# A hybrid S5 and mLSTM trunk on one core: where two weight blocks are staged, weight splits in pieces, and the step at which the W2 maxima are taken

## The chip, the cores and the metric

The kernel runs on one core of a Trainium2 chip. The metric is the device time of one execution in microseconds (us), of which the median over runs is taken. The engines are named as the profile does: PE (TensorE, matrix products), DVE (VectorE), ACT (ScalarE), POOL (GpSimd) and SP (SyncE, which here only issues DMAs).

## The reference

One layer of a streaming encoder on x of 2048 tokens by 1024 channels, float32. Its two mixers, S5 groups with a GLU and mLSTM heads, give 512 columns each:

```python
h = rmsnorm(x, norm_mix_g[l])
p = h @ w_in[l]
u, q_raw, k_raw, v, o_raw, i_raw, f_raw = jnp.split(p, cuts, axis=-1)
y_ssm = s5_mixer(u, ...)      # scan, GELU, z * sigmoid(z @ w_glu + b_glu), rmsnorm
y_ml = mlstm_mixer(q_raw, k_raw, v, o_raw, i_raw, f_raw, ...)
x = x + jnp.concatenate([y_ssm, y_ml], axis=-1) @ w_out[l]
h = rmsnorm(x, norm_ffn_g[l])
x = x + jnp.square(jax.nn.relu(h @ w_ff1[l])) @ w_ff2[l]
...
return rmsnorm(x, final_norm_g)
```

W_out is 1024 by 1024; W1 is 1024 by 4096 and W2 4096 by 1024.

## The kernel before

**Products.** Every float32 product is made of float16 parts: a weight w and an operand are each split into a high part and the rest (hi, lo), and three matmuls add up hi·hi, hi·lo and lo·hi (`mm3`, L160 to L162, and `mmx`, L1398 to L1400 in the FFN). So that the parts don't overflow, each weight block is first scaled by a power of two from the largest magnitude in it. Preparing a block is therefore: DMA of float32 into SBUF; the maximum of its magnitudes on DVE; a maximum over the partitions through PE and DVE (`all_max`, L94 to L101, tiles `pmx_...` and `ma_...`); some one-column steps; hi on ACT and lo on DVE.

**Mixers and the hand-over (to about 720 us).** The mixers go through 16 chunks of tokens. GLU steps (`glu_step(n)`, tiles `zc`, `pz`, `zt`, `pgl`, `gth`, `pgT`, `ms`; 128 tokens of one n at a time) run beside them and after them: `zt` is the split GLU input, `pgl` its product with W_glu, and `pgT` transposes the finished columns into `ms`, the operand of the output projection. The last chunk of the mLSTM (`og`, `pT`, `mo`, `mix_store`) fills the other half of it and writes it to DRAM (`ml_d`), from where it comes back as `hop0ml`, `hop1ml`. The output projection (`out_proj`, bank `po`, eight tiles of 128 output columns by 512 tokens, 24 matmuls each) adds its result to the x tiles `x2` (L1057).

**W_out** lies in four blocks of 256 columns. `load_wo(i)` calls `load_w` (L127 to L149), which takes a staging tile from the pool `stg` of one buffer (128 x 2048 float32, 1 MB), loads into it (L130), takes the maxima (`w_scale`, L107), and splits it in 8 pieces (L141 on ACT, L142 on DVE). Blocks 0 and 1 come during chunks 13 and 14 (L975, L977), block 2 before the last chunk's store (L979), and block 3 later, ahead of GLU step 9 (L1334). Two tiles of `po` use one block. The x tiles are four accumulators of 1 MB each, `accx`, tags `ax0` to `ax3`, loaded by `load_acc` (L1003 to L1005).

**FFN (about 830 to 2125 us).** Two phases over the halves of the tokens. A phase has 16 W1 blocks (numbered u below) of 128 x 2048 float32, each followed by its part of W2 (two halves of a load `r2`), in a scheme of seven products on sums of quarter blocks. Raw weights are combined on POOL (L1278 to L1281 for W1, L1319 to L1322 for W2), then split by `w_split` (L1263 to L1265: hi L1264 on ACT, lo L1265 on DVE) into `wA` and `wC` of 1024 columns, `wB` of 1536, and the `w2o` operands of 512 or 768. `f_scale` takes the maximum over the 2048 columns of one block (L1203 to L1212, tiles `m1_a..`, `m1_b..`, on DVE L1205) for those that aren't measured ahead; a stands for W1, b for W2. PE's results of the first product (`fx`, `fv`, `fw`) become the hidden operand (tiles `e..`, `t2f` L1101 and L1105, split on ACT L1090 and POOL L1091); the second (`gx`, `gv`, `gw`) is evacuated by DVE into the x tiles (L1494, in `f2_mp`), and only then does PE get its bank back. While phase 0 runs, DVE and POOL also prepare the operands of the second half of the tokens (tiles `b..`, L1142 to L1155, and `ho`), until about 1400 us.

`f2_mp` is a generator; for each quarter step qd and each product i of seven it issues the matmuls, the evacuations, and then at certain steps the preparation of what comes next: `w2_prep` of the next quarter step at i = 0, `w2_load` of the next pair of blocks at i = 1 of even qd, and `w2_scale` (which calls `f_scale`) of that pair at i = 6 of even qd.

**What sets the order.** The rows of all engines are set at build time by a scheduler that simulates the engines. So an edit in one place can move instructions elsewhere, and the order that came out is static.

Of the kernel before, what the change touches and what calls it, by code (L numbers as in the profile page):

```python
# [43 lines left out]
O_GMIX, O_GFFN, O_GFIN, O_GOUT, O_CW, O_CB, O_D, O_BI, O_BF, NCOL = 0, 8, 16, 24, 32, 64, 72, 104, 105, 106  # L44
# [3 lines left out]
def trunk(  # L48
# [18 lines left out]
    nc = tc.nc  # L67
    V, S, G, T = nc.vector, nc.scalar, nc.gpsimd, nc.tensor
# [7 lines left out]
    smal = ctx.enter_context(pool("smal", bufs=3))  # L76
# [50 lines left out]
    def load_w(src, K, N, ga, name, slot=0, wp=None, tag=None, E=V, st=None):  # L127
        if st is None:
            st = stg.tile([P, K, N], F32, name=f"st_{name}", tag="stg")
            nc.sync.dma_start(out=st, in_=src)  # L130
        wt = (wp or wpool).tile([P, 2, K, N], F16, name=f"w_{name}", tag=tag or f"w{slot}")
        sg, mp = w_scale(st, K, N, ga, name)
        if ga is not None and E is G:
            for k in range(K):
                V.tensor_scalar(out=st[:, k, :], in0=st[:, k, :], scalar1=sg[:, k:k + 1], scalar2=None, op0=ALU.mult)
                if k % 2 == 1:
                    S.activation(out=wt[:, 0, k - 1:k + 1], in_=st[:, k - 1:k + 1], func=AF.Copy)
                    G.tensor_tensor(out=wt[:, 1, k - 1:k + 1], in0=st[:, k - 1:k + 1], in1=wt[:, 0, k - 1:k + 1], op=ALU.subtract)
        elif ga is not None:
            for k in range(K):  # L140
                S.activation(out=wt[:, 0, k, :], in_=st[:, k, :], func=AF.Copy, scale=sg[:, k:k + 1])  # L141
                V.scalar_tensor_tensor(out=wt[:, 1, k, :], in0=st[:, k, :], scalar=sg[:, k:k + 1], in1=wt[:, 0, k, :], op0=ALU.mult, op1=ALU.subtract)  # L142
# [778 lines left out]

    wo, r_w = [None] * 4, [None] * 4

    def load_wo(i, slot=0, wp=None, tag=None):
        wo[i], m = load_w(wout[i], KD, 256, O_GOUT, f"out{i}", slot, wp, tag)
        r_w[i] = descale(m, 2.0 ** -24, f"out{i}", tag="dsw")

    mix_load(0)
# [7 lines left out]
    for b in range(16):  # L936
# [39 lines left out]
            load_wo(0, 2)  # L976
        if b == 14:  # L977
            load_wo(1, 0)
    load_wo(2, 1)  # L979
    mix_store(15)  # L980
    r_ctx.close()

# [214 lines left out]
    def sc1(name):  # L1197
        return scal.tile([P, 1], F32, name=name)
# [2 lines left out]

    def f_scale(raw, nm):

        m1 = smal.tile([P, 1], F32, name=f"m1_{nm}", tag="w_m1")
        V.tensor_reduce(out=m1, in_=raw, axis=AX.X, op=ALU.max, apply_absolute_value=True)  # L1205
        ma = all_max(m1, nm, *psx[nm[0]])
        mp = sc1(f"fm_{nm}")
        V.tensor_scalar(out=ma, in0=ma, scalar1=1e-30, scalar2=None, op0=ALU.max)
        V.tensor_scalar(out=mp.bitcast(I32), in0=ma.bitcast(I32), scalar1=0x7F800000, scalar2=None, op0=ALU.bitwise_and)
        sg = sc1(f"fs_{nm}")  # L1210
        V.reciprocal(sg, mp)
        V.tensor_scalar(out=sg, in0=sg, scalar1=4096.0, scalar2=None, op0=ALU.mult)  # L1212
        return mp, sg
# [47 lines left out]
                mp1["g", u // 2] = mg  # L1261

    def w_split(hi, lo, src, sg):  # L1263
        S.activation(out=hi, in_=src, func=AF.Copy, scale=sg)  # L1264
        V.scalar_tensor_tensor(out=lo, in0=src, scalar=sg, in1=hi, op0=ALU.mult, op1=ALU.subtract)  # L1265
# [31 lines left out]
    def w2_scale(ph, v):  # L1297
        raw = raw2[ph, v]
        if ph == 0:
            mp, sg2[v] = scanned.get(("b", v)) or f_scale(raw.rearrange("p m s n -> p (m s n)"), f"b{v}")  # L1300
            dd = dd2[v] = sc1(f"dd{v}")
            mg = mp1["g", v // 2]
            V.tensor_scalar(out=dd, in0=mg, scalar1=mg, scalar2=Mg2, op0=ALU.mult, op1=ALU.mult)
            V.tensor_scalar(out=dd, in0=dd, scalar1=mp, scalar2=None, op0=ALU.mult)

    def w2_prep(ph, q, wp=None, tag=None):
        v, j = q // 2, q % 2
        raw, sg = raw2[ph, v], sg2[v]
# [12 lines left out]
        G.tensor_tensor(out=r[:, 2], in0=r[:, 0], in1=r[:, 2], op=ALU.subtract)
        G.tensor_tensor(out=r[:, 1], in0=r[:, 1], in1=s12[:, 1], op=ALU.subtract)  # L1322
        w_split(fl(w[:, 0, 5:7]), fl(w[:, 1, 5:7]), fl(s12), sg)
        w_split(fl(w[:, 0, 2:5]), fl(w[:, 1, 2:5]), fl(r[:, 1:4]), sg)
        wops2[ph, q] = {n: w[:, :, i] for i, n in enumerate(("A11", "A12", "S4", "S3", "A22", "S1", "S2"))}


    def load_ml(t):
        mlr[t] = new_hop(t, f"ml{t}").rearrange("p a (b h) t -> p (a b) h t", h=2)
        nc.sync.dma_start(out=mlr[t], in_=ml_d[t])  # L1330

    load_ml(0)
    load_acc(0)
    load_wo(3, wp=r3, tag="wo3")  # L1334
    glu_step(9)
    for n in range(10, NGL):
        if n in (10, 12, 14):
            load_acc((n - 8) // 2)
        if n == 13:
            load_ml(1)  # L1340
        out_proj(0, n - 10)
        glu_step(n)
# [138 lines left out]
    def f2_mp(ph, g, mp, fam):  # L1481
        qd = 4 * g + mp
        nm = f"{ph}{qd}"
        dd = dd2[qd // 2]
        bk = {}
        acc = accx[mp]
        w = wops2[ph, qd]
        nq = (ph, qd + 1) if qd + 1 < 32 else (1, 0) if ph == 0 else None
        for i, (b, wn, op) in enumerate(PR2):
            if b not in bk:  # L1490
                bk[b] = bank(fam + b, f"g{b}{nm}")
            mmx(bk[b], [(w[wn][:, 0, f * P:(f + 1) * P], w[wn][:, 1, f * P:(f + 1) * P], hid[ph, 2 * g + f, op][:, 0, :], hid[ph, 2 * g + f, op][:, 1, :]) for f in range(2)], first=(i in (0, 1, 5)), last=True)
            for j, c in ((0, 0),) if i in (0, 5) else ((1, 1),) if i in (1, 4) else ((0, 1),) if i in (2, 3) else ((1, 0),):
                V.scalar_tensor_tensor(out=acc[:, j, c, :], in0=bk[b], scalar=dd, in1=acc[:, j, c, :], op0=ALU.mult, op1=ALU.add)  # L1494
            if i == 0 and nq:
                w2_prep(*nq)
            nv = (ph, qd // 2 + 1) if qd // 2 + 1 < 16 else (1, 0) if ph == 0 else None
            if i == 1 and qd % 2 == 0 and nv:
                w2_load(*nv)
            if i == 6 and qd % 2 == 0 and nv:  # L1500
                w2_scale(*nv)
            yield
        if ph == 0 and g == NFB // 2 - 1:
            for c in range(2):
                if accf[c] is None:
                    accf[c] = r3.tile([P, TB], F32, name=f"accf{ph}{c}", tag="acc", bufs=2)
# [198 lines left out]
```

## Time and profile before

| | |
|---|---|
| median of 3 runs | 2147.97 us (2147.96 to 2151.23) |
| the profiled execution | 2149.39 us |
| its span, first to last instruction | 2147.7 us |
| mean granted clock of TensorE | 0.979 |
| busy: PE, DVE, ACT, POOL | 2033.2, 1688.4, 1090.1, 1086.1 us |
| DMA | 176.57 MB, mean 82 GB/s |

A row of a timeline has the start in us, the length in us (for several instructions in a row, xcount, of them all), the engine, the line, the operation, what it writes and reads, its shape, and in brackets how long the engine was idle before it and what it was waiting for. Lines are those of the program above. A window has for each engine the busy time and the number of instructions in it, then the clock that TensorE was granted, the share of the DMA engines and their rate.

### The profile page before, as it was taken

The page shows a single profiled execution, that of the slowest core. Times are in us where ns is not written, and L with a number is a line of the kernel's source. Part 1 is how long each engine was busy: PE and PEld are TensorE (multiplying, and loading weights), DVE is VectorE, ACT ScalarE, POOL GpSimd, SP SyncE. Part 2 cuts the span into 40 slices and gives each one's busy share as a digit, 9 for nine tenths or more (in the row PEclk, how much of TensorE's full clock was granted, in tenths as well). Part 3 has the DMA queues.
Part 4 walks back from the last instruction along what each step waited for, and adds up shares of the span by engine and source line. Part 5 has one row for each costly group of instructions (what it writes and reads, how often), then busy time and mean ns, then how long its engine had stood idle before and what let it go on. Part 6 is the DMA issues. An engine that isn't in the chain of part 4 may idle for free.

```text
span 2147.7 us, 30032 instructions
## 1 busy us (share of the span) xinstructions
PE 2033.2 (95%) x11205; PEld 1160.0 (54%) x11205; DVE 1688.4 (79%) x2820; ACT 1090.1 (51%) x2078; POOL 1086.1 (51%) x988
## 2 busy tenths in 40 slices
PE   6999898998999799999999999999999999999996
PEld 4986776776667454444444444444444444444445
DVE  8878888887857766757988989987887887777776
ACT  6436555555545422365544554555655555555543
POOL 2124446453211102576765776685776567565645
PEclk9999999999999899999999999999999999999998
DMA  5112112211103342312222222125433232121112
GB/s 189 51 52 60 50 40 47 70 35 57 60 21 113 113 196 78 118 45 69 94 69 83 80 94 80 63 79 196 138 137 103 100 112 79 40 79 43 36 40 79
DMA packets 56883, 176.57 MB, mean 82 GB/s; under 512 B 8032, under 2 KB 21536, under 8 KB 43168
## 3 DMA queue, kind: packets, MB, share of 16 engines
q1 hardware_dynamic: 56736, 174.65, 24.1%
q8 instruction: 88, 1.44, 0.3%
q14 instruction: 59, 0.48, 0.1%
HBM read 137.83 MB, written 28.41 MB: 77 GB/s over the span
## 4 chain that ended last, share of the span: by engine, by line
PE 58%; DVE 23%; POOL 6%; DMA 5%; ACT 4%; issue 3%; SPq 1%; POOLq 0%; DVEq 0%; ACTq 0%
PE fx L1400 4%; PE fx L1398 3%; PE fx L1399 3%; PE gx L1398 3%; PE gx L1400 3%; PE gx L1399 3%; PE po L160 3%; PE po L162 3%; PE po L161 3%; DVE w2o L1265 2%; DMA r<-in_w_dram 2%; DVE x L1494 2%; PE fv L1400 2%; PE fv L1399 2%; PE fv L1398 2%
## 5 line engine op out<-in xcount | busy, mean ns | idle before, releaser
L1399 PEld LDWEIGHTS <-w2o 128*128 128x128 f16 x952 | 93.5, 98 | 125.8 <-issue 29.2
L1427 ACT ACTIVATE e<-e 128x512 f32<-128x512 f32 x96 | 60.3, 628 | 197.6 <-DVE e L1463 96.2
L1398 PEld LDWEIGHTS <-w2o 128*128 128x128 f16 x952 | 93.8, 98 | 104.4 <-issue 2.6
L1400 PEld LDWEIGHTS <-w2o 128*128 128x128 f16 x952 | 93.6, 98 | 103.7 <-DVE w2o L1265 2.4
L162 PE MATMUL pv<-w_vo,xn 128*128 128x256 f16 x512 | 142.5, 278 | 2.5 <-DVE vx L440 2.5
L160 PE MATMUL pv<-w_vo,xn 128*128 128x256 f16 x512 | 142.3, 278 | 1.0 <-ACT xn L449 1.0
L161 PE MATMUL pv<-w_vo,xn 128*128 128x256 f16 x512 | 142.3, 278 | 0.0
L1264 ACT ACTIVATE w2o<-r,fs_b 128x512 f16<-128x512 f32 (+1 forms) x96 | 78.9, 824 | 113.8 <-POOL r L1322 52.6
L1265 DVE SCALAR_TENSOR_TENSOR w2o<-r,fs_b,w2o 128x512 f16<-128x512 f32 (+1 forms) x96 | 103.9, 1084 | 26.1 <-ACT w2o L1264 25.7
L1322 POOL TENSOR_TENSOR r<-r,s 128x256 f32<-128x256 f32 x64 | 65.2, 1021 | 105.7 <-DVE w2o L1265 104.3
L1494 DVE SCALAR_TENSOR_TENSOR x2b<-gx,dd,x2b 128x512 f32<-128x512 f32 x112 | 82.8, 745 | 42.6 <-PE gx L1400 42.3
L1494 DVE SCALAR_TENSOR_TENSOR x<-gx,dd,x 128x512 f32<-128x512 f32 x128 | 94.4, 742 | 12.2 <-PE gx L1400 11.9
L1278 POOL TENSOR_TENSOR s<-r 128x512 f32<-128x512 f32 x32 | 52.8, 1650 | 91.5 <-issue 64.6
L160 PE MATMUL pq<-xn,w_qk 128*128 128x512 f16 x256 | 97.6, 382 | 0.0
L161 PE MATMUL pq<-xn,w_qk 128*128 128x512 f16 x256 | 97.6, 381 | 0.0
L162 PE MATMUL pq<-xn,w_qk 128*128 128x512 f16 x256 | 97.5, 381 | 0.0
L1398 PE MATMUL fx<-hop,wB 128*128 128x512 f16 x256 | 97.0, 379 | 0.1
L1399 PE MATMUL fx<-hop,wB 128*128 128x512 f16 x256 | 97.0, 379 | 0.0
L1400 PE MATMUL fx<-hop,wB 128*128 128x512 f16 x256 | 97.0, 379 | 0.0
L162 PEld LDWEIGHTS <-xn 128*128 128x128 f16 x768 | 88.0, 115 | 11.9 <-DVE vx L440 2.7
L160 PEld LDWEIGHTS <-xn 128*128 128x128 f16 x768 | 88.2, 115 | 11.3 <-ACT xn L449 1.7
L161 PEld LDWEIGHTS <-xn 128*128 128x128 f16 x768 | 88.2, 115 | 9.7 <-issue 0.7
(1373 smaller groups left out, 6948.6 us busy)
## 6 DMA issues: line engine op xcount, KB each, us to landing
r<-in_w_dram SPq DMA_DIRECT2D x64, 1024.0 KB, 5.0
xt<-in_xN_dram SPq DMA_DIRECT2D x16, 512.0 KB, 4.4
rt<-rh SPq DMA_DIRECT2D x64, 128.0 KB, 2.3
hopd<-ho SPq DMA_DIRECT2D x28, 256.0 KB, 2.5
hop<-hopd SPq DMA_DIRECT2D x7, 1024.0 KB, 5.0
st_vo<-in_wvo_dram SPq DMA_DIRECT2D x4, 1024.0 KB, 5.1
bcm<-negM_d SPq DMA_DIRECT2D x16, 256.0 KB, 3.2
ml_d<-mo SPq DMA_DIRECT2D x16, 256.0 KB, 2.3
```

The costliest lines, as they stand in the source:

```text
L160: T.matmul(out, wh, xh, start=(i == 0), stop=False)
L161: T.matmul(out, wh, xl, start=False, stop=False)
L162: T.matmul(out, wl, xh, start=False, stop=(i == n - 1))
L1264: S.activation(out=hi, in_=src, func=AF.Copy, scale=sg)
L1265: V.scalar_tensor_tensor(out=lo, in0=src, scalar=sg, in1=hi, op0=ALU.mult, op1=ALU.subtract)
L1278: G.tensor_tensor(out=s12[:, 0], in0=raw[:, 2], in1=raw[:, 3], op=ALU.add)
L1322: G.tensor_tensor(out=r[:, 1], in0=r[:, 1], in1=s12[:, 1], op=ALU.subtract)
L1398: T.matmul(out, wh, xh, start=(first and i == 0), stop=False, skip_group_check=True)
L1399: T.matmul(out, wh, xl, start=False, stop=False, skip_group_check=True)
L1400: T.matmul(out, wl, xh, start=False, stop=(last and i == n - 1), skip_group_check=True)
L1427: S.activation(out=x, in_=x if src is None else src, func=AF.Relu, scale=scale)
L1494: V.scalar_tensor_tensor(out=acc[:, j, c, :], in0=bk[b], scalar=dd, in1=acc[:, j, c, :], op0=ALU.mult, op1=ALU.add)
```

## The change

Three edits.

1. W_out blocks 2 and 3 no longer use the buffer `stg`. Two tiles of the tags `ax2` and `ax3` of the x accumulators take them; both are loaded by DMAs issued in front of `load_acc(0)`, and x tiles 2 and 3 load into these slots after the splits. `load_wo(2)` moves from ahead of `mix_store(15)` to behind it, `load_wo(3)` from ahead of `glu_step(9)` to behind it. The buffer `stg` is free for W1 block 0 earlier.
2. `f_scale` takes its maximum in two halves of 1024 columns and a third reduction over the two; `w_split` works in pieces of at most 512 columns (1024 in two, 1536 in three, 768 in 512 and 256), each with its ACT and DVE instruction.
3. In `f2_mp`, `w2_scale` moves from product 6 of an even quarter step to product 0 of the odd one after it, and `w2_prep` of the odd ones from product 0 to product 1.

```diff
-    def load_wo(i, slot=0, wp=None, tag=None):
-        wo[i], m = load_w(wout[i], KD, 256, O_GOUT, f"out{i}", slot, wp, tag)
+    def load_wo(i, slot=0, wp=None, tag=None, st=None):
+        wo[i], m = load_w(wout[i], KD, 256, O_GOUT, f"out{i}", slot, wp, tag, st=st)
...
-    load_wo(2, 1)
     mix_store(15)
...
     def f_scale(raw, nm):
 
+        mx = smal.tile([P, 8], F32, name=f"mx_{nm}", tag="w_mx")
+        for o in range(2):
+            V.tensor_reduce(out=mx[:, o:o + 1], in_=raw[:, 1024 * o:1024 * o + 1024], axis=AX.X, op=ALU.max, apply_absolute_value=True)
         m1 = smal.tile([P, 1], F32, name=f"m1_{nm}", tag="w_m1")
-        V.tensor_reduce(out=m1, in_=raw, axis=AX.X, op=ALU.max, apply_absolute_value=True)
+        V.tensor_reduce(out=m1, in_=mx[:, 0:2], axis=AX.X, op=ALU.max)
...
     def w_split(hi, lo, src, sg):
-        S.activation(out=hi, in_=src, func=AF.Copy, scale=sg)
-        V.scalar_tensor_tensor(out=lo, in0=src, scalar=sg, in1=hi, op0=ALU.mult, op1=ALU.subtract)
+        n = src.shape[-1]
+        for o in range(0, n, 512):
+            c_ = slice(o, min(o + 512, n))
+            S.activation(out=hi[:, c_], in_=src[:, c_], func=AF.Copy, scale=sg)
+            V.scalar_tensor_tensor(out=lo[:, c_], in0=src[:, c_], scalar=sg, in1=hi[:, c_], op0=ALU.mult, op1=ALU.subtract)
...
+    st_o = []
+    for i in (2, 3):
+        st_o.append(accxp.tile([P, KD, 256], F32, name=f"st_o{i}", tag=f"ax{i}"))
+        nc.sync.dma_start(out=st_o[-1], in_=wout[i])
     load_ml(0)
     load_acc(0)
-    load_wo(3, wp=r3, tag="wo3")
+    load_wo(2, 1, st=st_o[0])
     glu_step(9)
+    load_wo(3, wp=r3, tag="wo3", st=st_o[1])
...
-            if i == 0 and nq:
+            if qd % 2 == 0 and i == 0:
                 w2_prep(*nq)
...
-            if i == 6 and qd % 2 == 0 and nv:
-                w2_scale(*nv)
+            if qd % 2 == 1 and nq:
+                if i == 0:
+                    w2_scale(ph if qd < 31 else 1, nq[1] // 2)
+                elif i == 1:
+                    w2_prep(*nq)
```

The change moves rows on all engines. Lines after the edits are numbered a few higher in the changed program (L1265 is L1270 there, L1105 is L1104, L1494 is L1504). The first place is the hand-over. PE before, from the last products of GLU step 9 (`pgl9`) to the first output projection (`po00`):

```order
L913 MATMUL pT15_8163<-ident_72,og33_7898 128x128
L98 MATMUL pmx_gm_8195<-ident_72,gm_8193 128x128
L913 MATMUL pT15_8163<-ident_72,og33_7898 128x128 x3
L98 MATMUL pmx_out3_8220<-ident_72,m1_out3_8218 128x128
L806 MATMUL pgT7_8249<-ident_72,zc7_7791 128x128 x4
L160 LDWEIGHTS w_out0_7447
L160 MATMUL po00_8292<-ms0_6491,w_out0_7447 128x512
L160 LDWEIGHTS w_out0_7447
...
L775 MATMUL pz10_8258<-ident_72,zc10_8256 128x128 x4
L806 MATMUL pgT8_8320<-ident_72,zc8_7958 128x128 x4
L161 LDWEIGHTS w_out0_7447
L161 MATMUL po00_8292<-ms0_6491,w_out0_7447 128x512
```

And now:

```order
L913 MATMUL pT15_8126<-ident_72,og33_7898 128x128
L98 MATMUL pmx_gm_8158<-ident_72,gm_8156 128x128
L98 MATMUL pmx_out2_8185<-ident_72,m1_out2_8183 128x128
L913 MATMUL pT15_8126<-ident_72,og33_7898 128x128 x3
L806 MATMUL pgT7_8214<-ident_72,zc7_7791 128x128 x4
L160 LDWEIGHTS w_out0_7447
L160 MATMUL po00_8292<-ms0_6491,w_out0_7447 128x512
L160 LDWEIGHTS w_out0_7447
...
L775 MATMUL pz10_8223<-ident_72,zc10_8221 128x128 x4
L98 MATMUL pmx_out3_8260<-ident_72,m1_out3_8258 128x128
...
L161 MATMUL po00_8292<-ms0_6491,w_out0_7447 128x512
```

`pgT7`, which is followed by the first matmuls of the output projection, stood behind `pmx_out3`; now `pmx_out2` stands there, and `pmx_out3` comes after the transposes. DVE at the same place, where `zt9` is the operand of `pgl9`, before:

```order
L789 SCALAR_TENSOR_TENSOR gth8_8116<-pgl8_8103,zd_6522,bg_6514 128x512
...
L772 TENSOR_SCALAR zc9_8093<-uz1_1023,zs_6521 128x512
...
L791 SCALAR_TENSOR_TENSOR zc8_7958<-gth8_8116,zc8_7958 128x512
L810 TENSOR_TENSOR ms0_6491<-pgT6_8086,ms0_6491 128x8x64
...
L778 TENSOR_TENSOR zt9_8100<-pz9_8095,zt9_8100 128x512
...
L797 TENSOR_SCALAR zc8_7958<-zc8_7958,vg8_8120,zo_6523 128x512
...
L107 TENSOR_REDUCE mx_out3_8215<-st_out3_8212 128x8
...
L810 TENSOR_TENSOR ms0_6491<-pgT7_8249,ms0_6491 128x8x64
```

And now, with the maxima `mx_out2`, `mx_out3` and those of W1 block 0, `mx_a0`:

```order
L107 TENSOR_REDUCE mx_out2_8180<-st_o2_8171 128x8
L789 SCALAR_TENSOR_TENSOR gth8_8116<-pgl8_8103,zd_6522,bg_6514 128x512
...
L772 TENSOR_SCALAR zc9_8093<-uz1_1023,zs_6521 128x512
L107 TENSOR_REDUCE mx_out3_8255<-st_o3_8173 128x8
L1205 TENSOR_REDUCE mx_a0_8918<-r1_00_8809 128x1 x2
...
L895 SCALAR_TENSOR_TENSOR og33_7898<-og33_7898,pn151_8065 128x256
L810 TENSOR_TENSOR ms0_6491<-pgT6_8086,ms0_6491 128x8x64
L791 SCALAR_TENSOR_TENSOR zc8_7958<-gth8_8116,zc8_7958 128x512
L778 TENSOR_TENSOR zt9_8100<-pz9_8095,zt9_8100 128x512
...
L810 TENSOR_TENSOR ms0_6491<-pgT7_8214,ms0_6491 128x8x64
```

Three more reductions now stand ahead of the row that writes `zt9`, and no maximum of a weight block between it and the row that writes `ms0` from `pgT7`.

The second place is DVE in the FFN at W1 block 4, around the second `t2f04` row, which waits for POOL. Before:

```order
L1494 SCALAR_TENSOR_TENSOR x2_1_8289<-gx05_10951,dd2_10619,x2_1_8289 128x512
L1265 SCALAR_TENSOR_TENSOR wB05_10948<-r1_05_10379,sg_a4a5b2b3_9089,wB05_10948 128x1536
L1265 SCALAR_TENSOR_TENSOR w2o06_10959<-r2_03_10832,sg_a4a5b2b3_9089,w2o06_10959 128x512
L1494 SCALAR_TENSOR_TENSOR x2_1_8289<-gv05_10982,dd2_10619,x2_1_8289 128x512
L1265 SCALAR_TENSOR_TENSOR w2o06_10959<-s2_06_10962,sg_a4a5b2b3_9089,w2o06_10959 128x512
L1105 TENSOR_TENSOR t2f04_10898<-b2104_10938,t2f04_10898 128x512
L1155 TENSOR_TENSOR b41_0_10262<-b40_0_10757,b41_0_10262 128x512
L1494 SCALAR_TENSOR_TENSOR x2_1_8289<-gx05_10951,dd2_10619,x2_1_8289 128x512
L1205 TENSOR_REDUCE m1_a7_11033<-r1_07_10996 128x1
```

And now:

```order
L1504 SCALAR_TENSOR_TENSOR x2_1_8289<-gx05_11017,dd2_10700,x2_1_8289 128x512
L1270 SCALAR_TENSOR_TENSOR wB05_11010<-r1_05_10423,sg_a4a5b2b3_9100,wB05_11010 128x512
L1504 SCALAR_TENSOR_TENSOR x2_0_8177<-gx04_10854,dd2_10700,x2_0_8177 128x512
L1270 SCALAR_TENSOR_TENSOR wB05_11010<-r1_05_10423,sg_a4a5b2b3_9100,wB05_11010 128x512 x2
L1104 TENSOR_TENSOR t2f04_10963<-b2104_11000,t2f04_10963 128x512
L1154 TENSOR_TENSOR b41_0_10300<-b40_0_10818,b41_0_10300 128x512
L1270 SCALAR_TENSOR_TENSOR w2o06_11047<-r2_03_10897,sg_a4a5b2b3_9100,w2o06_11047 128x512
L1270 SCALAR_TENSOR_TENSOR w2o06_11047<-s2_06_11050,sg_a4a5b2b3_9100,w2o06_11047 128x512
L1504 SCALAR_TENSOR_TENSOR x2_1_8289<-gv05_11039,dd2_10700,x2_1_8289 128x512
L1270 SCALAR_TENSOR_TENSOR w2o06_11047<-r2_03_10897,sg_a4a5b2b3_9100,w2o06_11047 128x256
L1504 SCALAR_TENSOR_TENSOR x2_1_8289<-gx05_11017,dd2_10700,x2_1_8289 128x512
```

The two `w2o06` rows and the evacuation of `gv05` stood ahead of `t2f04` and now stand behind it, ahead of the evacuation of `gx05`. The third place is the same one of block 8. Before:

```order
L1265 SCALAR_TENSOR_TENSOR wB09_12244<-r1_09_11642,fs_a9_11691,wB09_12244 128x1536
L1494 SCALAR_TENSOR_TENSOR x2_0_8210<-gx012_12081,dd6_11909,x2_0_8210 128x512
L100 TENSOR_REDUCE ma_b7_12217<-pmx_b7_12215 128x1
L1208 TENSOR_SCALAR ma_b7_12217<-ma_b7_12217 128x1
L1105 TENSOR_TENSOR t2f08_12186<-b2108_12234,t2f08_12186 128x512
L1494 SCALAR_TENSOR_TENSOR x2_1_8289<-gv013_12278,dd6_11909,x2_1_8289 128x512
```

And now:

```order
L1270 SCALAR_TENSOR_TENSOR wB09_12363<-r1_09_11749,fs_a9_11801,wB09_12363 128x512 x3
L1504 SCALAR_TENSOR_TENSOR x2_0_8177<-gx012_12211,dd6_12059,x2_0_8177 128x512
L100 TENSOR_REDUCE ma_b7_12385<-pmx_b7_12383 128x1
L1504 SCALAR_TENSOR_TENSOR x2_1_8289<-gv013_12407,dd6_12059,x2_1_8289 128x512
L1210 TENSOR_SCALAR ma_b7_12385<-ma_b7_12385 128x1
L1211 TENSOR_SCALAR fm_b7_12387<-ma_b7_12385 128x1
L1104 TENSOR_TENSOR t2f08_12320<-b2108_12353,t2f08_12320 128x512
```

Here the evacuation of `gv013` stood behind `t2f08` and now stands ahead of it.

## The prediction

> **What bounds the kernel now.** I read the page's first part, then windows, the waits of PE, and the rows of single engines where PE stands. The page:
>
> ```profile
> span 2147.7 us, 30032 instructions
> PE 2033.2 (95%) x11205; PEld 1160.0 (54%) x11205; DVE 1688.4 (79%) x2820; ACT 1090.1 (51%) x2078; POOL 1086.1 (51%) x988
> ```
>
> PE is the bound: the change leaves its matmuls alone, so it can only move the 2147.7 − 2033.2 = 114.5 us in which PE idles, and matmuls that run at a lower clock. The windows (PE, PEld, DVE, ACT, POOL busy, granted clock, DMA share, GB/s) say where:
>
> ```profile
> 690.00:720.00 30.00, 15.48 (x70) 9.86 (x69) 22.16 (x68) 11.93 (x34) 2.60 (x4) 0.72 0.71 274
> 720.00:820.00 100.00, 100.00 (x498) 50.12 (x497) 68.95 (x111) 29.18 (x54) 10.69 (x11) 1.00 0.30 116
> 820.00:1060.00 240.00, 239.16 (x1122) 110.72 (x1120) 175.11 (x225) 116.73 (x176) 140.32 (x108) 1.00 0.25 85
> 1060.00:1400.00 340.00, 322.65 (x1474) 146.49 (x1473) 299.87 (x425) 168.53 (x249) 220.45 (x184) 0.98 0.24 78
> 1500.00:2060.00 560.00, 558.07 (x2590) 253.86 (x2588) 432.31 (x491) 294.46 (x427) 353.49 (x292) 1.00 0.24 83
> ```
>
> Two stretches matter: the hand-over from mixers to output projection (690 to 720, 14.5 us idle), and the FFN while VectorE still prepares the second half of the tokens (1060 to 1400, 17.35 us idle; DVE 299.87 of 340, with 40 to spare). Elsewhere in 720 to 2060 PE has almost no gap, so edits there can only cost. The waits of PE (us in total, times, longest), the first row over the span, the second in 1060 to 1400:
>
> ```profile
> PE pmx_out L98 <- DVE m_out L110: 8.2, 1, 8.2
> ...
> PE gx L1398 <- DVE x L1494: 11.6, 10, 3.6
> ```
>
> The price of a stall is more than its idle time. The largest of the FFN, from PE's rows and two windows:
>
> ```profile
> 1069.35 0.58 PE L1398 MATMUL gx<-hd02T,w2o 128*128 128x512 f16 x1 [3.61 <-DVE x L1494]
> 1069.72 0.63 PE L1399 MATMUL gx<-hd02T,w2o 128*128 128x512 f16 x1
> 1070.15 0.63 PE L1400 MATMUL gx<-hd02T,w2o 128*128 128x512 f16 x1
> ...
> 1060.00:1080.00 20.00, 16.39 (x65) 6.98 (x64) 16.45 (x27) 6.71 (x10) 12.08 (x11) 0.83 0.19 66
> 1500.00:1520.00 20.00, 20.00 (x95) 9.07 (x93) 15.06 (x18) 10.77 (x16) 12.96 (x13) 1.00 0.16 53
> ```
>
> After 3.61 us idle the matmuls start 0.43 us apart (1069.72 to 1070.15); the undisturbed window has 20/95 = 0.21. The disturbed one holds 65 instead of 95, so that stall cost 30 × 0.21 = 6.3 us, 1.75 times its idle time. By that factor the FFN stretch loses some 17.35 × 1.75 = 30 us; as most of its waits are shorter, I take 25.
>
> **Part 1: staging of W_out blocks 2 and 3.** Before, both went through the one buffer `st_out`. Block 3's load stands behind the splits of block 2:
>
> ```profile
> 684.33 0.33 SPq L130 DMA_DIRECT2D st_out<-in_wout_dram  x1
> ...
> 685.35 0.37 SPq L1330 DMA_DIRECT2D hop0ml<-ml_d  x1
> 688.38 1.42 SPq L1005 DMA_DIRECT2D x<-in_xT_dram  x3
> ...
> 707.91 0.34 SPq L130 DMA_DIRECT2D st_out<-in_wout_dram  x1
> ...
> 689.54 2.29 DVE L107 TENSOR_REDUCE mx_out<-st_out 128x8 f32<-128x2048 f32 x1 [0.91 <-DMA st_out<-in_wout_dram]
> ...
> 713.40 2.29 DVE L107 TENSOR_REDUCE mx_out<-st_out 128x8 f32<-128x2048 f32 x1 [2.08 <-DMA st_out<-in_wout_dram]
> ...
> 701.20 0.68 DVE L778 TENSOR_TENSOR zt<-pz,zt 128x512 f16<-128x512 f32 x1
> ...
> 716.23 0.77 PE L98 MATMUL pmx_out<-ident,m_out 128*128 128x128 f32 x2 [8.22 <-DVE m_out L110]
> 716.79 1.06 PE L806 MATMUL pgT<-ident,zc 128*128 128x128 f32 x4
> ...
> 720.54 0.38 PE L161 MATMUL po<-ms,w_out 128*128 128x512 f16 x1
> ```
>
> Issue 707.91, landing about 713.4, reduce until 715.7, `pmx_out` at 716.23. The transposes `pgT`, on which the first output projection hangs, stand behind `pmx_out` in PE's row though they don't need it. PE is gapless from 720.54, 3.75 after `pgT`.
>
> After, SP issues both loads behind the mixer's store, ahead of the x tiles. Their slots are those of x tiles 2 and 3, whose loads were issued in the batch at 688.38 (x3) and just after it, so they go at about 688.4. One MB from issue to landing took 689.54 − 684.33 = 5.2; for a megabyte queued right behind another I add half of that, 2.6 (by the 274 GB/s of the window it would be 3.8). Landings: 693.5 and 696.1. DVE then has, ahead of `zt` of GLU step 9: the maxima of block 2 until 695.8, of block 3 from its landing until 698.4, and of W1 block 0, which now loads into the freed `st_out` slot, in two pieces until 700.7; then steps that stood there before too, four of 512 columns at 0.66 (the pitch below) and small ones, 3.2 together. `zt` ends at 703.9, where it ended at 701.20 + 0.68 = 701.9: 2.0 later. PE idles there instead, and the ten `pgl` matmuls behind it, at 0.43 apart, take until about 708; the mixer's last transposes and `pmx_out2` until 709.3; then `pgT`. Hence `pgT` comes at 709.3 instead of 716.79: **7.5 us gained**. Bounds: 10 if `zt` isn't delayed (the 8.22 wait and its slow restart gone), 3.5 if both landings and the W1 maxima fall 4 us later (hop0ml and 2 MB of x share the queue).
>
> What is late next: the 16 splits of blocks 2 and 3 on DVE, now after `ms0`. Five of them took
>
> ```profile
> 719.14 2.08 DVE L142 SCALAR_TENSOR_TENSOR w_out<-st_out,sg_out,w_out 128x256 f16<-128x256 f32 x5
> ```
>
> so 16 take 6.7, ending near 720; block 2 is first read by the fifth tile of 24 matmuls, 4 × 24 × 0.21 = 20 us after the start. Nothing new there. x tiles 2 and 3 load only after the splits; their first adds stand over 50 us later, hidden. Were that cover gone, one landing of 5 us would show.
>
> **Part 2: pieces.** Pitch of DVE's splits with and without pieces:
>
> ```profile
> 1218.58 1.80 DVE L1265 SCALAR_TENSOR_TENSOR wB<-r,fs_a,wB 128x1536 f16<-128x1536 f32 x1
> 1220.31 0.74 DVE L1494 SCALAR_TENSOR_TENSOR x<-gx,dd,x 128x512 f32<-128x512 f32 x1
> ...
> 1226.08 0.75 DVE L1265 SCALAR_TENSOR_TENSOR w2o<-r,fs_b,w2o 128x512 f16<-128x512 f32 x1
> 1226.74 2.28 DVE L1205 TENSOR_REDUCE m_a<-r 128x1 f32<-128x2048 f32 x1
> ...
> 1073.66 1.26 DVE L1265 SCALAR_TENSOR_TENSOR wA<-r,fs_a,wA 128x1024 f16<-128x1024 f32 x1
> 1074.85 0.73 DVE L1494 SCALAR_TENSOR_TENSOR x<-gx,dd,x 128x512 f32<-128x512 f32 x1
> ```
>
> 512 columns take 0.66, 1024 take 1.19, 1536 take 1.73: each further piece costs 2 × 0.66 − 1.19 = 0.13. A W1 block (of 32 in some 1,300 us of FFN) has four more, its two W2 halves one each: 6 × 0.13 = 0.78 per 40 us. In 1060 to 1400 that is 8.5 × 0.78 = 6.6 on DVE, against 40 to spare; from 1500 DVE has 128 to spare. ACT's pieces lie beside a 50% idle engine. So in itself **0**, bounded by 0 and 6.6. What pieces allow is an evacuation (L1494) between two of them; a wB was 1.80 in front of one.
>
> **Part 3: order in the FFN.** Moving the W2 maxima and the pieces reshuffles DVE's row. The stalls before came where DVE waits for POOL at `t2f` with evacuations queued behind it:
>
> ```profile
> 1061.80 1.67 DVE L1265 SCALAR_TENSOR_TENSOR w2o<-s,sg_a4a5b2b,w2o 128x512 f16<-128x512 f32 x1
> 1065.88 1.62 DVE L1105 TENSOR_TENSOR t2f<-b,t2f 128x512 f32<-128x512 f32 x1 [2.41 <-POOL hd04T L1091]
> 1067.43 1.20 DVE L1155 TENSOR_TENSOR b<-b,b 128x512 f32<-128x512 f32 x1
> 1068.56 0.74 DVE L1494 SCALAR_TENSOR_TENSOR x<-gx,dd,x 128x512 f32<-128x512 f32 x1
> ...
> 1222.55 1.63 DVE L1105 TENSOR_TENSOR t2f<-b,t2f 128x512 f32<-128x512 f32 x1 [1.12 <-POOL hd08T L1091]
> 1224.10 0.74 DVE L1494 SCALAR_TENSOR_TENSOR x<-gv,dd,x 128x512 f32<-128x512 f32 x1
> ```
>
> At block 4 two W2 pieces and the evacuation of gv, before ahead of the wait, now stand behind it and ahead of gx: 2 × 0.66 + 0.66 + a quarter piece 0.4 = 2.4 later (4 if POOL stretches the pieces as at 1061.80), with slow restart 3 to 4 us lost. At block 8 the evacuation of gv now stands ahead of `t2f` (1.12 + 1.63 sooner), at block 10 likewise: 2 × 1.7 of stall and restart gained. At block 12 gx's evacuation goes behind one FFN evacuation, the W1 maxima and W2 pieces (0.66 + 2.3 + 1.3): 3 to 4 lost if PE is already there, none if it isn't, since wB lets gx through earlier. At the others I see no clear side. Sum: −3.4 + 3.5 + 0 to 4, say **0**; bounds −8 (a third of the 25 us goes) and +12.
>
> The last stretch (2060 to the end) has only smaller pieces: 0, at most 1 either way.
>
> **A rule against the pieces.** The rows of DVE operations with minimum, median and longest time in ns:
>
> ```profile
> L1265 DVE SCALAR_TENSOR_TENSOR wB<-r,fs_a,wB x24: 1801/1819/2799, 819.9 to 2034.2; 128x1536 f16<-128x1536 f32 x24
> L1105 DVE TENSOR_TENSOR t2f<-b,t2f x32: 674/1530/1744, 947.0 to 2076.5; 128x512 f32<-128x512 f32 x32
> L1205 DVE TENSOR_REDUCE m_a<-r x12: 2268/2280/2287, 727.8 to 1381.9; 128x1 f32<-128x2048 f32 x12
> ```
>
> Operations with two SBUF inputs are stretched by up to 1.0 us, once, whatever their length; maxima never. The Trainium skill, page "SBUF — State Buffer", section "Who interferes with whom", says that VectorE with two SBUF inputs contends with a GpSimd instruction that reads SBUF, that the shared port pair is an exclusive lock held for a whole instruction, and that a reduction does not contend. The rows agree, and by the rule each piece asks for the lock anew.
>
> **The rivals.**
> 1. *The FFN gains too.* Pieces let evacuations through and blocks 8 and 10 are only the plain cases. For: the 10 waits of gx average 1.2, less than one wB. Against: block 4. A third of 25: −8 more, so 2140.5 − 8 = 2132.5.
> 2. *Evacuations end up behind pieces* (slower). Place: blocks 4, 6 and 12, where DVE waits for POOL at `t2f` and gx's evacuation is behind W2 pieces. Each loses about 4 us, so +12, net +4.5: 2152.5. It decides the sign when the FFN loses more than 7.5. Against: each such wait must find PE already waiting.
> 3. *Every piece pays the lock.* In 1060 to 1400 8.5 × 6 = 51 more pieces; if a third pay 1.0, DVE has 17 + 6.6 less of its 40, and the stalls grow by about half of 17.35 to +8: net 0, 2148.5.
> 4. *The staging gain is eaten*: `zt` of step 9 held until 708 by late landings and three maxima; 3.5 instead of 7.5, and the FFN no better: 2144.5 to 2147.
>
> **How the numbers follow.** The profiled execution took 2149.39 (its span and 1.7 around it), 1.4 above the median 2147.97; sums are taken off the median. Forecast: 2147.97 − 7.5 + 0 = 2140.5. Chances: forecast 0.43 (2136 to 2144), rival 1 0.19, rival 4 0.14, rival 3 0.09, rival 2 0.15. About 0.2%, 4.3 us, can be told apart. Faster takes the forecast but its slow edge and rival 1: 0.59. Same takes rival 4, most of rival 3 and that edge: 0.24. Slower takes rival 2 and the rest: 0.17. The range reaches from below rival 1 to rival 2: 2130 to 2153.
>
> **What would show it.** Right: no wait of `pmx_out` over 1 us, `pgT` of step 7 near 709, a new idle of some 5 us before the twelve `pgl`, PE gapless from about 713; in 1060 to 1400 idle between 13 and 22 with a `t2f` stall at block 4 longer than 3.6. Wrong: a wait of `po` for `w_out` or of `xo` for x tiles after 713; FFN idle under 10 (rival 1) or over 25 (rival 2); medians of 512-column splits over 1.0 us (rival 3).

## The result and the profile after

The changed kernel takes 2176.39 us (median; 2175.25 to 2177.1) against 2147.97: the ratio is 1.0135, with a 95% interval of 1.0122 to 1.0147. It is 28 us slower where 7.5 us faster was forecast. The page's head of the profiled execution (2177.1 us):

```profile
span 2175.3 us, 30477 instructions
PE 2042.9 (94%) x11205; PEld 1158.4 (53%) x11205; DVE 1763.5 (81%) x3060; ACT 1124.3 (52%) x2270; POOL 1059.0 (49%) x988
```

PE's matmuls are the same in number; DVE has 240 more instructions and is busy 1763.5 − 1688.4 = 75.1 us longer. The windows that answer to those of before:

```profile
690.00:720.00 30.00, 20.62 (x101) 10.72 (x101) 25.01 (x64) 11.90 (x33) 6.45 (x6) 0.83 0.61 233
720.00:820.00 100.00, 100.00 (x498) 50.15 (x497) 71.18 (x119) 30.88 (x60) 7.03 (x8) 1.00 0.38 142
820.00:1060.00 240.00, 235.85 (x1101) 108.56 (x1101) 182.60 (x255) 121.65 (x203) 142.11 (x115) 1.00 0.24 81
1060.00:1400.00 340.00, 311.52 (x1405) 139.62 (x1405) 305.31 (x479) 171.42 (x290) 202.24 (x172) 0.98 0.23 76
1400.00:2060.00 660.00, 647.41 (x2987) 293.04 (x2986) 550.35 (x712) 361.82 (x603) 403.42 (x349) 1.00 0.27 93
```

The hand-over got through 101 matmuls in place of 70. The FFN lost: from 820 to 1060 there are 1101 matmuls where there were 1122, from 1060 to 1400 1405 where there were 1474, and from 1400 to 2060, where before had next to no gap, 2987 in place of this:

```profile
1400.00:2060.00 660.00, 658.07 (x3056) 299.78 (x3055) 514.01 (x594) 349.62 (x509) 423.52 (x353) 1.00 0.27 93
```

The last two stretches are 69 matmuls short each. At 660/3056 = 0.216 us for one, that is 15 us each, and 4.5 us for the 21 of the first. PE idles 28.5 us from 1060 to 1400, where it was 17.35. Its waits there, of which before 11.6 of 16.7 us were of gx for DVE:

```profile
PE gx L1408 <- DVE x L1504: 10.8, 12, 2.5
PE pmx_a L98 <- DVE m_a L1207: 7.1, 3, 3.0
PE gv L1408 <- DVE x L1504: 4.3, 3, 2.1
PE fx L1408 <- ACT e L1455: 4.3, 1, 4.3
PE gw L1408 <- DVE ma_b L100: 1.9, 2, 1.5
```

PE waits for DVE at more places, and also for the maxima of W1 blocks, whose matmul (`pmx_a`) stands in its row. Two places in the FFN show what DVE does meanwhile, first at 1302, then in the second phase at 1618, each with the wait of PE that ends there:

```profile
1302.02 3.86 DVE L1270 SCALAR_TENSOR_TENSOR wB<-r,fs_a,wB 128x512 f16<-128x512 f32 x3
1305.81 0.74 DVE L1504 SCALAR_TENSOR_TENSOR x<-gv,dd,x 128x512 f32<-128x512 f32 x1
...
1306.60 0.38 PE L1408 MATMUL gv<-hd08B,w2o 128*128 128x512 f16 x1 [2.08 <-DVE x L1504]
...
1618.32 4.33 DVE L1270 SCALAR_TENSOR_TENSOR wB<-r,sg_a2a3b0b,wB 128x512 f16<-128x512 f32 x3
1622.58 0.74 DVE L1504 SCALAR_TENSOR_TENSOR x2b<-gv,dd,x2b 128x512 f32<-128x512 f32 x1
...
1623.37 0.54 PE L1408 MATMUL gv<-hd10B,w2o 128*128 128x512 f16 x1 [2.27 <-DVE x2b L1504]
```

Three pieces of a wB take 3.86 and 4.33 us one behind the other, where one whole wB took 1.82 as a rule and 2.80 at most; the evacuation of gv stands behind them, and PE behind that. The pieces take 2.0 and 2.5 us more than a whole wB of 1.82, and PE's waits are 2.08 and 2.27. The pieces of wB and the 256-column pieces of W2 by their shapes (busy, mean ns of one), and wB's with shortest, median and longest:

```profile
L1270 DVE SCALAR_TENSOR_TENSOR wB<-r,fs_a,wB 128x512 f16<-128x512 f32 x72 | 81.0, 1158 | 4.0 <-ACT wB L1269 3.9
...
L1270 DVE SCALAR_TENSOR_TENSOR wB<-r,fs_a,wB x72: 736/1186/1654, 810.9 to 2063.5; 128x512 f16<-128x512 f32 x72
...
L1270 DVE SCALAR_TENSOR_TENSOR w2o<-r,fs_b,w2o 128x256 f16<-128x256 f32 x48 | 48.5, 1011 | 0.0
```

A 512-column piece of wB takes 1.16 us in the mean and 0.74 at the shortest, a 256-column piece 1.01 in the mean. The pieces of wA and wC, by the same views, take 0.82 and 0.75 in the mean, so hardly more than the shortest.

Since a profiled execution can be a few us ahead or behind already before 690, I compare kernels by two stretches that don't hold that: the **hand-over**, from the last matmul of `pv` in the mixers to the last of `po`, and the **FFN**, from there to the first matmul on `hd112T` (block 12 of the second phase). The starts in the profiles of before and after:

```profile
688.08 0.27 PE L162 MATMUL pv<-w_vo,xn 128*128 128x256 f16 x1
...
911.98 0.38 PE L162 MATMUL po<-ml,w_out 128*128 128x512 f16 x1
...
2019.01 0.38 PE L1398 MATMUL gx<-hd112T,w2o 128*128 128x512 f16 x1
```

```profile
687.04 0.27 PE L162 MATMUL pv<-w_vo,xn 128*128 128x256 f16 x1
...
904.94 0.38 PE L162 MATMUL po<-ml,w_out 128*128 128x512 f16 x1
...
2045.40 0.38 PE L1408 MATMUL gx<-hd112T,w2o 128*128 128x512 f16 x1
```

The hand-over went from 223.9 to 217.9, 6.0 less; the FFN from 1107.0 to 1140.5, 33.4 more.

### The profile page after: what moved, and what is told of

The parts are those of the page before. It is cut to its first block, busy times and chain, and to the rows that moved or that the text cites. A ratio compares the mean times of both kernels' runs of the same rounds, so it can differ in the third digit from the quotient of the medians.

```text
span 2175.3 us, 30477 instructions
## 1 busy us (share of the span) xinstructions
PE 2042.9 (94%) x11205; PEld 1158.4 (53%) x11205; DVE 1763.5 (81%) x3060; ACT 1124.3 (52%) x2270; POOL 1059.0 (49%) x988
## 4 chain that ended last, share of the span: by engine, by line
PE 49%; DVE 31%; DMA 6%; POOL 4%; ACT 4%; issue 4%; SPq 1%; POOLq 0%; DVEq 0%; ACTq 0%
DVE w2o L1270 5%; DMA r<-in_w_dram 4%; DVE x L1504 3%; PE gx L1408 3%; DVE wB L1270 3%; PE po L160 3%; PE po L162 3%; PE gx L1410 3%; PE po L161 3%; PE gx L1409 3%; PE fx L1410 3%; PE fx L1408 3%; PE fx L1409 3%; DVE y L248 2%; PE fv L1408 1%
## 5 line engine op out<-in xcount | busy, mean ns | idle before, releaser
L1269 ACT ACTIVATE w2o<-r,fs_b 128x512 f16<-128x512 f32 (+1 forms) x144 | 92.2, 643 | 129.7 <-POOL r L1327 74.1
L1270 DVE SCALAR_TENSOR_TENSOR w2o<-r,fs_b,w2o 128x512 f16<-128x512 f32 (+1 forms) x144 | 137.0, 955 | 9.1 <-ACT w2o L1269 9.0
L1504 DVE SCALAR_TENSOR_TENSOR x2b<-gx,dd,x2b 128x512 f32<-128x512 f32 x112 | 82.8, 743 | 44.7 <-PE gx L1410 44.4
L1504 DVE SCALAR_TENSOR_TENSOR x<-gx,dd,x 128x512 f32<-128x512 f32 x128 | 94.6, 740 | 11.0 <-PE gx L1410 10.9
L1283 POOL TENSOR_TENSOR s<-r 128x512 f32<-128x512 f32 x32 | 46.1, 1440 | 95.7 <-issue 85.1
```

The lines of the kernel that those rows point to most:

```text
L1269: S.activation(out=hi[:, c_], in_=src[:, c_], func=AF.Copy, scale=sg)
L1270: V.scalar_tensor_tensor(out=lo[:, c_], in0=src[:, c_], scalar=sg, in1=hi[:, c_], op0=ALU.mult, op1=ALU.subtract)
L1283: G.tensor_tensor(out=s12[:, 0], in0=raw[:, 2], in1=raw[:, 3], op=ALU.add)
```

## The experiments

Theory L: VectorE's lo splits have two SBUF inputs and share a port with POOL; each instruction pays for it anew, so pieces multiply the price, and DVE's longer row holds up PE's evacuations. Rivals: O, the scheduler's new order and the moved or halved maxima are at fault; A, ACT's pieces are; O2, the order that the scheduler made of the pieces, and not their price.

**One part alone.** `e1_stage` is the kernel before with only the first edit (`load_wo`, `st_o`) of the diff.

> Staging of W_out blocks 2 and 3 alone, FFN edits undone. Both theories: the hand-over gives what it gave in the changed kernel, first lo-part matmul of po near 713.5 instead of 720.5, so 7 us less: 2141 (2138 to 2144), ratio 0.997. If it comes out at 2148 or more, the FFN's loss has a part in the staging (order or late x tiles).

Measured: 2140.76 us, ratio 0.9967 (0.9954 to 0.9979). Hand-over 218.7, FFN 1106.8: 5.2 less and 0.2 less. The staging by itself has no part in the loss. The start of `po` was a miss: the profiled execution came to the hand-over 2.7 us later, and its lo-part matmul stood at 718.01, which is 5.2 sooner counted from `pv`.

`e2_pieces` has only the new `w_split`:

```diff
+        n = src.shape[-1]
+        for o in range(0, n, 512):
+            c_ = slice(o, min(o + 512, n))
+            S.activation(out=hi[:, c_], ...)
+            V.scalar_tensor_tensor(out=lo[:, c_], ...)
```

> Only the splits in pieces of 512. Theory L (each piece pays for the port that DVE shares with POOL): most of the 35 us lost in the FFN is here, 2148 + 25 to 35 = 2173 to 2183, DVE busy 50 to 70 us more, the mean of wB's 512 pieces near 1.15 us and of w2o's 256 pieces near 1.0. Theory O (order: maxima late, PE held at pmx_a, evacuations behind them): pieces alone cost at most 5, 2148 to 2153.

Measured: 2179.3 us, ratio 1.0150 (1.0123 to 1.0176); FFN 1131.7, 24.7 more. Its page and its pieces:

```profile
PE 2036.4 (94%) x11205; PEld 1158.6 (53%) x11205; DVE 1757.9 (81%) x3012; ACT 1124.9 (52%) x2270; POOL 1057.3 (49%) x988
...
L1268 DVE SCALAR_TENSOR_TENSOR wB<-r,fs_a,wB 128x512 f16<-128x512 f32 x72 | 78.7, 1130 | 4.2 <-ACT wB L1267 4.1
...
L1268 DVE SCALAR_TENSOR_TENSOR w2o<-r,fs_b,w2o 128x256 f16<-128x256 f32 x48 | 46.6, 971 | 0.0
```

DVE is busy 69.5 us longer with 192 more instructions, 0.36 each, not the 0.13 of the forecast. Most of the loss is in this edit: of the FFN's 33.4 us it shows 24.7.

`e3_halves` has only the new `f_scale`.

> Only the maxima of f_scale in two halves. Theory L: reductions were never stretched, so 24 blocks cost 24 x 0.3 = 7 us of DVE and no time: 2148 plus or minus 3. Theory O: 10 or more slower, with waits of pmx_a for m_a on PE as in the changed kernel.

Measured: 2152.53 us, ratio 1.0018 (1.0007 to 1.0028), FFN 3.5 more, DVE 1688.4, as before. The 7 us of DVE did not come, and the time is a little above the range. A small loss, without more work: its longest wait of PE between 1400 and 1500, where before had none, is this:

```profile
1431.47 0.38 PE L1401 MATMUL gx<-hd010T,w2o 128*128 128x512 f16 x1 [2.67 <-DVE x L1497]
```

Of waits of `pmx_a` for `m_a`, 7.1 us in the changed kernel, there was one of 1.7 us.

`e4_move` has only the two moved conditions in `f2_mp`.

> Only the W2 maxima at the later step. Theory L: the same work in another place, 2148 plus or minus 4. Theory O: 10 or more slower; w2o arrives later and PE waits for gv or gx behind it.

Measured: 2147.79 us, ratio 0.9995 (0.9984 to 1.0007), FFN 1106.5. Nothing. O falls as the main cause: the halved and the moved maxima give 3 us together.

**Which pieces.** `e5_dve_pieces` writes each hi whole and only lo in pieces; `e6_act_pieces`, whose edit stands here, the other way round, with 9999 for 512 and 512 for 9999.

```diff
+        n = src.shape[-1]
+        for o in range(0, n, 512):
+            c_ = slice(o, min(o + 512, n))
+            S.activation(out=hi[:, c_], in_=src[:, c_], func=AF.Copy, scale=sg)
+        for o in range(0, n, 9999):
+            c_ = slice(o, min(o + 9999, n))
+            V.scalar_tensor_tensor(out=lo[:, c_], in0=src[:, c_], scalar=sg, in1=hi[:, c_], op0=ALU.mult, op1=ALU.subtract)
```

> Kernel before, with only DVE's lo parts in pieces of 512; ACT writes each hi part whole. Theory L (each DVE piece pays for the port shared with POOL): nearly all of the 30 us remains, 2170 to 2182, DVE busy 60 to 70 us above before. Theory A (ACT's pieces, in front of ACT's other work, hold up fx and the hidden operands): at most 10 slower, 2148 to 2158.

Measured: 2172.76 us, ratio 1.0112 (1.0097 to 1.0127); DVE 1758.0.

> Kernel before, with only ACT's hi parts in pieces of 512; DVE's lo parts whole. Theory L: no loss, 2148 plus or minus 4. Theory A: 20 to 30 slower, 2168 to 2178.

Measured: 2145.17 us, ratio 0.9981 (0.9972 to 0.9991), FFN 1101.9, 5.1 less. ACT's pieces alone are a gain, so A falls; DVE's carry the loss.

`e7_wB_pieces` cuts only sources of 1536 columns, `e8_w2_pieces` only those of 768.

> Kernel before, with only wB (1536 columns) in three pieces, 64 more pieces. Theory L: DVE 30 to 36 us more, about half of the 69 of all pieces, so about half of the loss: 2160 to 2166. Theory O2 (the loss comes from the order that the scheduler made of the whole, not from the pieces' price): not proportional, anywhere from 2145 to 2180, with DVE busy up by the fixed cost of 8 us only.

Measured: 2154.3 us, ratio 1.0025 (1.0016 to 1.0035), DVE 1713.8, 25 more. The price on DVE is there, smaller than expected; the time rose by 5 to 6, not 12 to 18.

> Kernel before, with only the 768 columns of a W2 part in 512 and 256, 64 more pieces. Theory L: the 256 pieces take about 1.0 us each though 0.47 alone, DVE 25 to 33 us more, a good third of the loss: 2157 to 2164. Theory O2: not proportional, DVE up by 8 us only.

Measured: 2160.12 us, ratio 1.0054 (1.0039 to 1.0069), DVE 1728.1, 40 more. So the same number of pieces costs twice as much time here, and the time goes with what DVE gained (25 and 40), but not in proportion. O2's sign, 8 us more of DVE, failed in both; its other sign, that the time isn't proportional, did not. Together the two runs have 65 of the 69.5 us that DVE gained in `e2_pieces`, but by the ratios only 17 of its 32 us (`e5_dve_pieces`: 24). The rest of the time lies with the pieces of wA and wC, which no run has alone, or with the order of the whole. The shapes:

```profile
L1268 DVE SCALAR_TENSOR_TENSOR w2o<-r,fs_b,w2o 128x256 f16<-128x256 f32 x48 | 44.6, 928 | 0.0
```

**The price by itself.** `e9_port_alone` computes nothing of the reference. It runs DVE's splits once alone and once beside POOL:

```diff
+    for kind, n, m in ((1536, 8, 0), (1536, 8, 30), (512, 24, 0), (512, 24, 44), (256, 24, 0), (256, 24, 36), (0, 8, 0), (0, 8, 14)):
...
+        for o in range(m):
+            G.tensor_tensor(out=z2[...], in0=z0[:, 0:256], in1=z1[:, 0:256], op=ALU.subtract)
+        for o in range(n):
+            V.scalar_tensor_tensor(out=lo[:, c_], in0=r[:, c_], scalar=sc, in1=hi[:, c_], op0=ALU.mult, op1=ALU.subtract)
```

> The disputed cost by itself; nothing of the reference is computed, the output is a filler. Stretches on DVE: 8 lo splits of 1536 columns, 24 of 512, 24 of 256, 8 maxima of 1024, each once alone and once beside a stream of POOL subtractions of 128x256 float32 with both inputs in SBUF. Theory L (a lock for a whole instruction): the stretch is per instruction, about the same 0.4 to 1.0 us for 1536, 512 and 256 columns, so three pieces beside POOL cost 1 to 2 us more than one; maxima unchanged. Theory P (the port is shared out by the column): the stretch goes with the columns, 256 gets a sixth of what 1536 gets, and pieces cost nothing beyond 0.13 each.

DVE's timeline, each kind alone and then beside POOL (start, time of all in the row):

```profile
7.89 14.80 DVE L108 SCALAR_TENSOR_TENSOR lo<-r,sc,hi 128x1536 f16<-128x1536 f32 x8
...
23.85 17.65 DVE L108 SCALAR_TENSOR_TENSOR lo<-r,sc,hi 128x1536 f16<-128x1536 f32 x8
...
57.54 15.98 DVE L108 SCALAR_TENSOR_TENSOR lo<-r,sc,hi 128x512 f16<-128x512 f32 x24
...
74.58 26.71 DVE L108 SCALAR_TENSOR_TENSOR lo<-r,sc,hi 128x512 f16<-128x512 f32 x24
...
116.64 9.58 DVE L108 SCALAR_TENSOR_TENSOR lo<-r,sc,hi 128x256 f16<-128x256 f32 x24
...
127.28 20.32 DVE L108 SCALAR_TENSOR_TENSOR lo<-r,sc,hi 128x256 f16<-128x256 f32 x24
...
157.61 10.00 DVE L110 TENSOR_REDUCE mx<-r 128x1 f32<-128x1024 f32 x8
...
168.78 10.00 DVE L110 TENSOR_REDUCE mx<-r 128x1 f32<-128x1024 f32 x8
```

and POOL's, beside the 512-column splits and beside the maxima:

```profile
74.63 40.87 POOL L104 TENSOR_TENSOR z<-z,z 128x256 f32<-128x256 f32 x44
...
168.72 9.61 POOL L104 TENSOR_TENSOR z<-z,z 128x256 f32<-128x256 f32 x14
```

Beside POOL an instruction takes longer by 2.85/8 = 0.36 us at 1536 columns, 10.73/24 = 0.45 at 512 and 10.74/24 = 0.45 at 256: the price goes with the instruction, not with its columns. A wB in three pieces takes 3 × 1.11 = 3.34 in place of 2.21. Alone, the same columns took 14.80 whole and 15.98 in pieces, 1.18/16 = 0.07 for each further piece. Maxima pay nothing. The two engines take turns, as this count says: a POOL subtraction takes 9.61/14 = 0.69 beside maxima; POOL had the time from 101.3, when DVE's 24 splits ended, to 115.5 for itself, 14.2/0.69 = 20.6 of its 44, so 23.4 of them fell beside the 24 splits, one for each. The Trainium skill, page "SBUF — State Buffer", section "Who interferes with whom", has it so: the pair of ports is locked for a whole instruction, and a reduction never contends. This run agrees that the price is one of the instruction and that a maximum pays none. But a split and a subtraction together take 1.11, and not 0.67 + 0.69 = 1.36: some 0.25 us of them still overlap.

**The partner taken away.** `e10_before_no_combos` is the kernel before without the four `G.tensor_tensor` of `w1_prep` and of `w2_prep` each; `e11_pieces_no_combos` is the same with the new `w_split`.

> Kernel before without POOL's combinations of raw weights (four subtractions or additions per W1 block and per W2 part left out; the splits take raw columns in their place). This is the base for the next kernel. Both theories: lo splits near their shortest times (wB 1.82, w2o of 768 near 1.0), fewer waits of DVE for POOL: 2125 to 2145.

> The same without POOL's combinations, with all splits in pieces of 512. Theory L: with POOL's largest stream gone the pieces lose most of their price: DVE no more than 25 to 35 us above the kernel without combinations (69 with them), 256 pieces below 0.7 us, and the time 0 to 8 above it (30 with them). If the loss stays at 20 or more, the port isn't the cause, and the order is.

Measured: 2128.69 us (ratio to the kernel before 0.9903, 0.9880 to 0.9926) and 2138.49 (0.9944, 0.9926 to 0.9962). The pages:

```profile
PE 2027.7 (95%) x11205; PEld 1159.8 (55%) x11205; DVE 1650.6 (78%) x2820; ACT 1086.6 (51%) x2078; POOL 678.4 (32%) x604
```

```profile
PE 2027.7 (95%) x11205; PEld 1157.7 (54%) x11205; DVE 1695.0 (79%) x3012; ACT 1119.5 (52%) x2270; POOL 649.5 (30%) x604
...
L1268 DVE SCALAR_TENSOR_TENSOR w2o<-r,fs_b,w2o 128x256 f16<-128x256 f32 x48 | 34.1, 710 | 0.0
```

With POOL busy 678 us in place of 1086 the pieces cost 9.8 us (from two and three runs), not 30, and DVE 44.4 more, not 69.5: 0.23 for a piece in place of 0.36. Both are above what was expected: POOL still splits the hidden operands (L1091), and a 256 piece still takes 0.71, where the shortest take 0.47. The direction is L's, and DVE's price shows it directly. The time shows it less: without the combinations no split waits for them, and in `e10_before_no_combos` PE idles only 2.5 us from 1060 to 1400, so a longer row of DVE has fewer waits to lengthen. How much of the remaining 9.8 is port and how much is the fixed price is not separated.

**A better version.** `e12_stage_act_pieces` joins the first edit with the ACT half of `w_split`, and leaves the rest as before.

> A candidate: staging of blocks 2 and 3, and only ACT's hi parts in pieces of 512; DVE's splits, the maxima and their step as before. If the two gains add up (7 to 8 from the staging, 3 to 4 from ACT's pieces): 2137 (2133 to 2141), ratio 0.995. If the shorter hand-over moves the scheduler's order in the FFN, only the 7 of the staging: 2141.

Measured: 2137.74 us, ratio 0.9939 (0.9922 to 0.9955), FFN 1101.0. The two gains, 7.1 and 4.1 us by their ratios, add up within the noise to its 13.1. It beats both kernels.

## Why the prediction was wrong, step by step

**Part 1, the staging, was right.** The forecast was 7.5 (3.5 to 10); the trace has 6.0 in the changed kernel and 5.2 alone, the times of `e1_stage` 7.1 (0.33% of 2148, interval 4.5 to 9.9). The steps, from DVE's and PE's rows of the changed kernel:

```profile
694.07 2.29 DVE L107 TENSOR_REDUCE mx_out<-st_o 128x8 f32<-128x2048 f32 x1 [2.43 <-DMA st_o<-in_wout_dram]
...
697.47 2.28 DVE L107 TENSOR_REDUCE mx_out<-st_o 128x8 f32<-128x2048 f32 x1
699.67 2.33 DVE L1205 TENSOR_REDUCE mx_a<-r 128x1 f32<-128x1024 f32 x2
...
703.58 0.68 DVE L778 TENSOR_TENSOR zt<-pz,zt 128x512 f16<-128x512 f32 x1
...
709.81 0.66 PE L806 MATMUL pgT<-ident,zc 128*128 128x128 f32 x4
...
713.49 0.38 PE L161 MATMUL po<-ms,w_out 128*128 128x512 f16 x1
```

The first landing was foretold for 693.5 and came at 694.07, `zt` for 703.9 and ended at 704.26, `pgT` for 709.3 and came at 709.81. This execution came to the hand-over 1.0 us earlier (687.04 against 688.08), so counted from `pv` each step is some 1.5 us later than foretold, and `pgT` is 5.9 us sooner than before, not 7.5. The order of the steps was right, and PE's new idle in front of the twelve `pgl`, foretold as some 5 us, was 4.3. The wait for `pmx_out` is gone, and the W_out splits and late x tiles hold nobody up.

**Part 2, the pieces, is the step that failed.** It priced a further piece at 0.13 us of DVE, from pitches of splits that ran undisturbed, and set it at nothing because DVE had 40 and 128 us to spare. Both were wrong. A piece cost 0.36 in the kernel (`e2_pieces`). That is a mean: the pieces of wB and the 256-column ones were stretched, those of wA and wC hardly. In `e9_port_alone` a split alone pays nothing, and beside a steady POOL stream every one, whole or piece, pays 0.36 to 0.45, since about one POOL instruction gets its turn for each. And spare time of DVE is no slack of its row: `wB` in three stretched pieces lies ahead of an evacuation that PE waits for, at 1302 as at 1618, the latter in a stretch where PE had been gapless and 128 us were counted as cover. The stretch from 1400 to 2060 has nearly half of the loss. That the other waits come about in the same way is argued from these two places; no run keeps the order of DVE's row and changes the price alone.

**The rule was there, and its price was about right.** Rival 3 had the mechanism, "Every piece pays the lock". Its price for DVE, 17 + 6.6 us on 51 pieces, is 0.46 for a piece, a little above the measured 0.36. What it had wrong was what that does to PE: it looked at 1060 to 1400 alone, set 40 us of spare time against it, let the stalls grow by 8 us at most, and came out at no change with a chance of 0.09. So the cover failed even where the price held. The forecast's own price could have been better, too. A whole wB seldom paid (median 1.82, shortest 1.80), and Part 2 read one undisturbed w2o row of 512 columns. The group of such rows before, with shortest, median and longest, and then the mean:

```profile
L1265 DVE SCALAR_TENSOR_TENSOR w2o<-s,fs_b,w2o x48: 734/758/1762, 1107.0 to 2098.2; 128x512 f16<-128x512 f32 x48
...
L1265 DVE SCALAR_TENSOR_TENSOR w2o<-s,fs_b,w2o 128x512 f16<-128x512 f32 x48 | 53.9, 1122 | 0.0
```

The mean is 0.39 above the shortest, near the 0.36 that a piece was to cost. The median, 0.02 above the shortest, hides that: half of the rows are hardly stretched, and the longest by 1.0. What would have shown the forecast wrong named the pieces too: medians of 512-column pieces over 1.0. The median of wB's is 1.19, that of wA's 0.74.

**Part 3, the order in the FFN**, was set at 0 with bounds of −8 and +12; the moved maxima gave 0 (`e4_move`), the halved ones 3.5 (`e3_halves`). The stall foretold at block 4 came in another form (PE waited 4.3 us for fx there, behind ACT). The idle of 28.5 us from 1060 to 1400 is above 25, the sign named for rival 2. Reading single places of the order told nothing on the sum. Rival 2, the one on the slower side, put evacuations behind pieces as it happened, but as three places at `t2f`, with +12 in place of +33.

**What adds up and what stays open.** Parts alone, from the ratios: −7.1 + 32 + 3.9 − 1.1 = 28 us, against 28.4 (29 by the ratio) for the whole. In the FFN of the profiled executions they give 27.5 of 33.4. Not settled: why halved maxima cost 3 to 4 us with no more work; where the 15 us are that the pieces of wB and of the 768 columns leave over; and whether ACT's pieces, a gain of 4 alone, are a loss beside DVE's pieces (2179.3 against 2172.8, but the intervals of the ratios overlap, and the FFN takes some 1131.7 in both profiled executions). The order of DVE's row differs between all of these, but no run separates that.

## What to carry to other kernels

Before cutting an operation into pieces, look for what each piece pays again: take the mean against the shortest duration of an operation that is already as short as the pieces, and if the long ones run beside another engine, charge the difference to every piece. Idle time of a busy in-order engine is no cover for work that stands ahead of what the bounding engine waits for. Cut on the engine whose pieces hold nobody up, here ACT (31.6 us more busy in `e6_act_pieces`, and a faster kernel), and leave the other's operation whole.

## What the runs showed of the hardware

A two-input SBUF split on DVE pays about 0.36 to 0.45 us for a steady POOL stream whether it has 256, 512 or 1536 columns, so the 256-column split more than doubles (0.40 to 0.85) while the 1536-column one grows by a fifth (1.85 to 2.21). About one POOL instruction got in for each DVE instruction, so POOL pays as well: while DVE did its 24 splits of 512 columns in 26.7 us, POOL got through some 23 subtractions (worked out above), which beside maxima take 16. Maxima on DVE pay nothing: 8 took 10.00 us alone and beside POOL.
